# A decoder layer on one core: q and b of the input projection computed as units with the activation in the array, and the gates on the same activation

## The chip, the cores and the metric

The kernel runs on one core of one Trainium2 chip. TensorE (PE) multiplies; VectorE (DVE) and ScalarE (ACT) prepare its operands and take its results out of the accumulators; SyncE (SP) and GpSimd (POOL) issue transfers. A matmul holds a block of 128 by 128 of one operand in the array (the stationary one) and streams the other past it (the moving one). The metric is the device time of one execution in microseconds; 2173.79 us is the median of three runs of the kernel before (2173.52 to 2174.09).

## What is computed

One decoder layer on 256 tokens with 16 learned meta tokens ahead of them (272 rows of 2048 values), all in float32:

```python
s = s + 0.5 * swiglu_ffn(rms_norm(s, norm_ffn1), ffn1_w_gu, ffn1_w_down)
h = rms_norm(s, norm_mix)
q, k, v, b_gate, c_gate, u = split(h @ w_in)            # 6 x 1024 columns
y_att  = rms_norm(softmax(q1 k1) v - lam * softmax(q2 k2) v, subln)   # 8 heads, causal
y_conv = b_gate * conv3(c_gate * u)
gates  = sigmoid(h @ w_gate)                             # 2 x 2048 columns
s = s + (gates[0] * (y_att @ w_branch[0]) + gates[1] * (y_conv @ w_branch[1])) @ w_out
s = s + 0.5 * swiglu_ffn(rms_norm(s, norm_ffn2), ffn2_w_gu, ffn2_w_down)
return rms_norm(s, norm_final)[16:]
```

## The kernel before

Every float32 operand of a large product is split into a high part, which the fast float32 form of the array takes exactly, and a low remainder: ACT casts the high part (`wh` of a weight tile), DVE subtracts it (`wl`). A product is then three matmuls: high by high, high by low, low by high.

There are two forms of a linear layer. In the dense form, `linear`, a weight block of 128 by 128 is stationary and the activation streams: 272 columns in three matmuls where the meta tokens are needed (k, v and the first feed-forward part), 258 columns (c and u), or for 256 tokens one matmul of 512 columns (both parts of the activation side by side) and one of 256 (q, b and the output projection). One call covers 512 output columns: 16 chunks of 128 rows by 4 blocks, 192 or 128 matmuls. In the unit form, `linear_mix`, activation blocks of 128 tokens are stationary and 512 columns of weights stream. A unit covers 1024 output columns and goes through eight pairs of chunks. A pair of kind D takes two tiles of 12 matmuls. A pair of kind S saves an eighth: it uses sums of activation blocks (`Mixed.combine`, kept in the tiles `sp`) and of weight blocks (the tiles `t`, lines 566 to 568) and takes 21 matmuls in four tiles. The plan "DDDSDSDS" of the gates has 5 x 24 + 3 x 21 = 183 matmuls. The results of a unit have tokens on the partitions; where the next step wants channels there, 128 by 128 blocks are transposed back on TensorE (`back`).

The order of the mixer before: k, q, v for heads 0 to 3, k, q, v for heads 4 to 7 (dense calls), then c, u, b twice, then four times a unit of gates and `z`, the product with the branch weights. The gates need an activation of 256 tokens in blocks of 128. Its normed copy `hn` is made chunk by chunk during u and b of the second half (`renorm`, lines 462 to 476), with the sums of its three S pairs.

Work that is not part of a layer's own stream stands in lists. `side` holds steps that a linear pops at fixed chunks (`side_at`): the 18 attention steps, their norm, the eight output transposes, the second half of the convolution. An attention step for one head and one half of the tokens does three things (lines 816 to 866): `values` of the unit two back, `turn` (transposes on TensorE) of the unit one back, `scores` of its own, whose softmax then runs through DVE, ACT and DVE and must be done when the next step transposes it. `pending` holds the evaluation of the layer before, run at chunk 1 of the next one; `later` holds transposes back. The written order is then put through a scheduler that interleaves each engine's instructions; each engine runs its own list in order. SP loads weight tiles of 1 MB into a ring of four (`st`), and `wh` and `wl` have rings of three tiles, so ACT and DVE prepare a tile at most three ahead of TensorE. The eight PSUM banks are one pool.

SBUF: one pool of 24 buffers of 4352 bytes (tag `act`) holds the activations, the attention's tensors and held weights. The pool `sc` has two buffers of 2176 bytes, for softmax tiles, sums and single 512-column weight tiles of the S pairs. The addresses of one of its two buffers are 128 bytes away, modulo 256, from those of all other streamed weight tiles, and the first tile (`wh`) of each S pair's single product lies there.

## Time and profile before

| | |
|---|---|
| median of the runs (lowest to highest) | 2173.79 us (2173.52 to 2174.09) |
| the profiled execution, its own time | 2175.27 us |
| its span, first to last instruction | 2173.5 us |
| mean granted clock of TensorE | 0.998 |
| busy: PE, DVE, ACT, POOL | 99%, 71%, 50%, 4% |

The stages of the profiled execution, from the first matmul of each name to the first of the next:

| stage | from us | to us |
|---|---|---|
| first feed-forward part | 7.0 | 810.1 |
| k, q, v of heads 0 to 3 | 810.1 | 881.2 |
| k, q, v of heads 4 to 7 | 881.2 | 964.3 |
| c, u, b, first half | 964.3 | 1048.4 |
| c, u, b, second half | 1048.4 | 1118.7 |
| gates and z, four times | 1118.7 | 1375.2 |
| output projection | 1375.2 | 1467.7 |
| second feed-forward part and the end | 1467.7 | 2173.5 |

How to read the lines: in a view of groups, a row has the line of the kernel, the engine, the operation, the tile written and the tiles read, the shapes, the count, the total and the mean time of one, then the idle time just before and what ended it. In a timeline a row has start, length and instruction. In a table of windows it has the stretch, its length and the busy time and number of instructions of each engine; PEld is TensorE's weight load, which runs beside the matmuls. Instructions overlap a little at their ends, so what one costs in a packed row is the distance between starts, which is less than its length.

### The profile page before, as it was taken

To read this page: it belongs to the slowest core of one execution; us is meant where nothing else is said; L and a number is where in the kernel's file an instruction comes from. 1 tells how busy PE (TensorE), PEld (TensorE's weight loads), DVE (VectorE), ACT (ScalarE), POOL (GpSimd) and SP (SyncE) were. 2 spreads that over 40 slices of the span, in tenths; PEclk is the share of its full clock that TensorE was granted. 3 is DMA by queue.
4 is the path that set the end of the run, shared out by engine and by line. 5 is a ranking of instruction groups with operands and counts; after the bars stand their busy time and mean duration, and the time that the engine had idled before them with its cause. 6 is when DMAs were issued, how large, how long until landed. Compare 5 with 4: busy or idle time off the path is not lost.

```text
span 2173.5 us, 33436 instructions
## 1 busy us (share of the span) xinstructions
PE 2161.5 (99%) x13459; PEld 1961.4 (90%) x13459; DVE 1553.4 (71%) x2060; ACT 1082.9 (50%) x1366; POOL 82.5 (4%) x93
## 2 busy tenths in 40 slices
PE   9999999999999999999999999999999999999998
PEld 9999999999999999999988888888888888888886
DVE  7555554445555555567897778678998899988997
ACT  6343343333433444445555555456665566555664
POOL 0000000000000000000000000001110111002100
PEclk9999999999999999999999999999999999999999
DMA  7555555555555555544556567557886999779964
GB/s 248 181 175 175 175 178 175 175 175 175 175 175 175 175 175 175 175 137 138 182 184 202 197 200 222 197 183 232 272 253 207 275 290 281 231 222 290 285 222 155
DMA packets 209313, 440.77 MB, mean 203 GB/s; under 512 B 10557, under 2 KB 11270, under 8 KB 209158
## 3 DMA queue, kind: packets, MB, share of 16 engines
q1 hardware_dynamic: 192214, 398.13, 54.7%
q0 software_dynamic: 16480, 39.85, 8.4%
q8 instruction: 105, 1.72, 0.3%
q10 hardware_dynamic: 464, 0.66, 0.1%
q14 instruction: 50, 0.41, 0.1%
HBM read 431.26 MB, written 2.10 MB: 199 GB/s over the span
## 4 chain that ended last, share of the span: by engine, by line
PE 96%; DVE 2%; DMA 1%; issue 1%; ACT 0%; POOL 0%; SPq 0%; DVEq 0%; ACTq 0%; POOLq 0%
PE pg L528 6%; PE pg L529 6%; PE pg L530 6%; PE pu L323 4%; PE pd L321 4%; PE pd L323 4%; PE pu L321 4%; PE pg L323 4%; PE pu L322 4%; PE pd L322 4%; PE pg L321 4%; PE pg L322 4%; PE o L319 3%; PE g L528 2%; PE g L529 2%; PE g L530 2%
## 5 line engine op out<-in xcount | busy, mean ns | idle before, releaser
L310 DVE TENSOR_TENSOR wl<-st,wh 128x1024 fp32r<-128x1024 f32 (+1 forms) x393 | 479.5, 1222 | 439.4 <-ACT wh L305 438.5
L305 ACT CAST wh<-st 128x1024 fp32r<-128x1024 f32 (+1 forms) x392 | 411.1, 1049 | 603.8 <-PE pd L322 147.2
L424 DVE TENSOR_TENSOR wl<-st,wh 128x1024 fp32r<-128x1024 f32 (+1 forms) x360 | 402.3, 1124 | 59.0 <-ACT wh L423 56.9
L423 ACT CAST wh<-st 128x1024 fp32r<-128x1024 f32 (+1 forms) x360 | 341.8, 974 | 195.5 <-PE pdx L529 45.0
L423 ACT CAST wh<-t 128x1024 fp32r<-128x1024 f32 x130 | 135.8, 1052 | 182.6 <-DVE t L568 114.3
L321 PE MATMUL pg<-h,wh 128*128 128x272 f32 x704 | 203.6, 290 | 1.2 <-ACT h L193 1.2
L321 PE MATMUL pu<-h,wh 128*128 128x272 f32 x704 | 203.1, 289 | 0.0
L321 PE MATMUL pd<-m,wh 128*128 128x272 f32 x704 | 203.1, 288 | 0.0
L323 PE MATMUL pd<-m,wl 128*128 128x272 f32 x704 | 203.0, 288 | 0.0
L323 PE MATMUL pu<-h,wl 128*128 128x272 f32 x704 | 203.0, 288 | 0.0
L322 PE MATMUL pg<-h,wh 128*128 128x272 f32 x704 | 202.5, 288 | 0.1
L322 PE MATMUL pu<-h,wh 128*128 128x272 f32 x704 | 202.4, 288 | 0.0
L322 PE MATMUL pd<-m,wh 128*128 128x272 f32 x704 | 202.4, 288 | 0.0
L323 PE MATMUL pg<-h,wl 128*128 128x272 f32 x704 | 201.7, 290 | 0.2 <-DVE wl L310 0.2
L424 DVE TENSOR_TENSOR wl<-t,wh 128x1024 fp32r<-128x1024 f32 x130 | 158.1, 1223 | 48.1 <-ACT wh L423 43.2
L529 PE MATMUL pg<-wh,h 128*128 128x512 f32 x399 | 156.3, 392 | 0.0
L530 PE MATMUL pg<-wl,h 128*128 128x512 f32 x399 | 156.1, 391 | 0.0
L528 PE MATMUL pg<-wh,h 128*128 128x512 f32 x399 | 155.7, 390 | 0.0
L321 PEld LDWEIGHTS pg<-h,wh 128*128 128x128 f32 x704 | 132.7, 189 | 2.0 <-ACT h L193 1.4
L322 PEld LDWEIGHTS pg<-h,wh 128*128 128x128 f32 x704 | 133.2, 189 | 0.4 <-DVE h L194 0.4
L323 PEld LDWEIGHTS pg<-h,wl 128*128 128x128 f32 x704 | 132.1, 189 | 0.8 <-DVE wl L310 0.6
L322 PEld LDWEIGHTS pu<-h,wh 128*128 128x128 f32 x704 | 132.7, 189 | 0.0
(327 smaller groups left out, 4880.4 us busy)
## 6 DMA issues: line engine op xcount, KB each, us to landing
st<-in_ffn_w_gu_dram SPq DMA_DIRECT2D x183, 512.0 KB, 5.8
st<-in_ffn_w_down_dram SPq DMA_DIRECT2D x88, 1024.0 KB, 5.2
st<-in_ffn_w_gu_dram SPq DMA_DIRECT2D x84, 1024.0 KB, 5.1
st<-in_w_in_dram SPq DMA_DIRECT2D x48, 1024.0 KB, 5.1
st<-in_w_gate_dram SPq DMA_DIRECT2D x64, 512.0 KB, 4.6
t<-in_ffn_w_gu_dram POOLq DMA_DIRECT2D x64, 512.0 KB, 6.8
st<-in_w_branch_dram SPq DMA_DIRECT2D x32, 512.0 KB, 5.4
st<-in_w_out_dram SPq DMA_DIRECT2D x16, 1024.0 KB, 5.1
```

What stands on the lines that cost most here:

```text
L305: nc.scalar.copy(out=wh[:, :m, :], in_=sw)
L310: nc.vector.tensor_sub(wl[:, :m, :], sw, wh[:, :m, :].bitcast(F32))
L319: nc.tensor.matmul(acc[j][:, : 2 * n], wh[:, i, f], act.both(c, t0, t1), start=first, stop=False)
L321: nc.tensor.matmul(a, wh[:, i, f], act.part(c, 0, t0, t1), start=first, stop=False)
L322: nc.tensor.matmul(a, wh[:, i, f], act.part(c, 1, t0, t1), start=False, stop=False)
L323: nc.tensor.matmul(a, wl[:, i, f], act.part(c, 0, t0, t1), start=False, stop=last)
L423: part_last[:] = [nc.scalar.copy(out=wh, in_=src).ins]
L424: part_last.append(nc.vector.tensor_sub(wl, src, wh.bitcast(F32)).ins)
L528: nc.tensor.matmul(ps[k], hi, wh, start=first, stop=False)
L529: nc.tensor.matmul(ps[k], lo, wh, start=False, stop=False)
L530: nc.tensor.matmul(ps[k], hi, wl, start=False, stop=left[k] == 0)
```

## The change

Five things are changed together.

1. q and b are no longer four dense calls of 512 columns. Each is one unit of 1024 columns, run after the first k in the order q, b, with the gates' plan of pairs (`Q_B`). The unit's results have tokens on the partitions. They are transposed back in eight sets of four 128 by 128 transposes (`turned_back`): q's four during b, b's four during the v that follows. q's norm factor moves into the scores' scale (`rq`), b's into four ACT multiplications. A norm factor with tokens on the partitions is made for it (`end_tok`).
2. The gates and the two new units read `h2`, the activation that k, v, c and u stream. `renorm` and `hn` go. The sums of the three S pairs are made from `s` while the feed-forward part ends. The sigmoid gets the norm factor as its scale.
3. Addresses: each piece of `h2` has 320 columns, of which the last 272 are used, so that the token blocks start 256 bytes into a piece, at the same residue modulo 256 as the weight tiles. `sc` gets buffers of 2304 bytes and `lam` is padded to 192 bytes, so that both buffers of `sc` lie at that residue too. The 24 buffers become 16 of 4352 bytes and 8 of 5120 bytes (tag `big`).
4. The attention has fewer dense calls to stand in. Five steps each stand in the second k and the second v, three chunks apart; in c and u they are three chunks apart as before. The output transposes are done two heads at a time.
5. What b's call evaluated, the product with the convolution, follows the convolution's second half: in c of the second half, and in the first pair of the first gates.

The second half of the w_in stage is thus k, v, c, u, c, u.

In TensorE's list, where q begins. Names: `h` is the activation, `wh` and `wl` the weight parts, `q`, `qx` and `k` PSUM banks. Before:

```order
L323 MATMUL k_8521<-h_131,wl 128x272
L319 MATMUL q_8790<-h_124,wh 128x512
L323 MATMUL q_8790<-h_124,wl 128x256
L319 MATMUL q_8791<-h_124,wh 128x512
L323 MATMUL q_8791<-h_124,wl 128x256
```

In the changed kernel, at the same place:

```order
L331 MATMUL k_8544<-h_131,wl 128x272
L522 MATMUL q_8855<-wh,h_124 128x512
L523 MATMUL q_8855<-wh,h_124 128x512
L524 MATMUL q_8855<-wl,h_124 128x512
L522 MATMUL q_8859<-wh,h_124 128x512
L523 MATMUL q_8859<-wh,h_124 128x512
```

and further on in b, where the first part of q is turned back (`qb_ps` is its bank):

```order
L523 MATMUL bx<-wh,h_125 128x512
L524 MATMUL bx<-wl,h_125 128x512
L780 MATMUL qb_ps<-ident,cgate 128x128 x4
L522 MATMUL b_9183<-wh,h_125 128x512
L523 MATMUL b_9183<-wh,h_125 128x512
```

Where a matmul of 512 and one of 256 columns stood for each weight block, three of 512 stand for each pair of an activation block and 512 weight columns, and sets of four transposes stand between them.

In DVE's list, a wide attention unit (272 columns of scores) in the second dense call after the first v (before, q of heads 4 to 7), the softmax between `sc_ps` and `rs`:

```order
L826 SCALAR_TENSOR_TENSOR sc<-sc_ps,mask 128x272 x2
L830 TENSOR_REDUCE mx<-sc 128x2
L837 RECIPROCAL rs<-sm 128x2
L838 TENSOR_TENSOR rs<-rs,lam 128x1
L839 TENSOR_SCALAR sc<-sc,rs 128x272
L840 SCALAR_TENSOR_TENSOR sc<-sc,rs 128x272
L310 TENSOR_TENSOR wl<-st,wh 128x1024
```

and the first wide unit of the changed kernel, in the second k:

```order
L846 SCALAR_TENSOR_TENSOR sc<-sc_ps,rq,mask 128x272 x2
L850 TENSOR_REDUCE mx<-sc 128x2
L318 TENSOR_TENSOR wl<-st,wh 128x1024
L857 RECIPROCAL rs<-sm 128x2
L858 TENSOR_TENSOR rs<-rs,lam 128x1
L859 TENSOR_SCALAR sc<-sc,rs 128x272
L860 SCALAR_TENSOR_TENSOR sc<-sc,rs 128x272
```

A weight tile's subtraction has moved into the middle of the softmax.

In DVE's list at the head of the first gates (`yv` and `cg` belong to the convolution, `yc` is the split result, `t` the weight sums of the first S pair). Before:

```order
L950 TENSOR_TENSOR yv_11087<-half,yv_11087 128x256 x2
L187 TENSOR_TENSOR yc_10131<-yv_11087,yc_10131 128x2x256
L424 TENSOR_TENSOR wl<-st,wh 128x1024
L187 TENSOR_TENSOR yc_10132<-yv_11087,yc_10132 128x2x256
L424 TENSOR_TENSOR wl<-st,wh 128x1024
L566 TENSOR_TENSOR t_12023<-st 128x1024
```

In the changed kernel:

```order
L963 SCALAR_TENSOR_TENSOR yv_11253<-cg,vec,yv_11253 128x256
L970 TENSOR_TENSOR yv_11253<-yv_11253,bT_9556 128x1024
L432 TENSOR_TENSOR wl<-st,wh 128x1024
L195 TENSOR_TENSOR yc_10535<-yv_11253,yc_10535 128x2x256
L195 TENSOR_TENSOR yc_10536<-yv_11253,yc_10536 128x2x256
L560 TENSOR_TENSOR t_11935<-st 128x1024
```

b's evaluation has gone from this place; the whole convolution of the second half (taps of four channel groups, L959 to L963) and its product with `bT` stand there now, ahead of the same weight sums.

The diff, cut to its core:

```diff
-N_ACT = 24
+N_ACT = 16
+N_BIG = 8
+PIECE = 320
...
-GATES = ("DDDSDSDS", 2, {(2, 1): 3, (4, 1): 5, (6, 1): 7}, ())
-FFN2_FIRST = ("DDDDSSDS", 1, {(3, 0): 4, (3, 1): 5, (6, 0): 7}, (4, 5))
-FFN2 = ("DDSDSSDS", 1, {(1, 1): 2, (3, 0): 4, (3, 1): 5, (6, 0): 7}, (2, 4, 5))
-DOWN_FIRST = ("DDDDDDSD", 1, {(5, 1): 6}, ())
-DOWN = ("DDSDSDSD", None, {(1, 1): 2, (3, 1): 4, (5, 1): 6}, ())
-DOWN_LAST = ("DDDSDS", 1, {(2, 1): 3, (4, 1): 5}, ())
+GATES = ("DDDSDSDS", (2,), {(2, 1): 3, (4, 1): 5, (6, 1): 7}, ())
+Q_B = ("DDDSDSDS", (1, 2), {(2, 1): 3, (4, 1): 5, (6, 1): 7}, ())
...
-    lam = const.tile([P, 1], F32, name="lam")
+    lam = const.tile([P, 48], F32, name="lam")[:, 0:1]
...
     class Act:
-        def __init__(self, name, chunks, width):
-            self.width = width
-            self.tiles = [
-                apool.tile([P, 2, 2, width], F32R, tag="act", name=f"{name}{g}") for g in range(chunks // 2)
-            ]
+        def __init__(self, name, chunks, width, wide_slots=(), piece=None):
+            self.width, self.lead = width, 0 if piece is None else piece - width
+            self.tiles = []
+            for g in range(chunks // 2):
+                if g in wide_slots:
+                    w = piece or width
+                    raw = apool.tile([P, 4 * PIECE], F32R, tag="big", bufs=N_BIG, name=f"{name}{g}")
+                    self.tiles.append(raw[:, : 4 * w].rearrange("p (c l w) -> p c l w", c=2, l=2))
+                else:
+                    self.tiles.append(apool.tile([P, 2, 2, width], F32R, tag="act", name=f"{name}{g}"))
         def both(self, c, t0, t1):
-            return self.tiles[c // 2][:, c % 2, :, t0:t1]
+            return self.tiles[c // 2][:, c % 2, :, self.lead + t0 : self.lead + t1]
         def part(self, c, lo, t0, t1):
-            return self.tiles[c // 2][:, c % 2, lo, t0:t1]
+            return self.tiles[c // 2][:, c % 2, lo, self.lead + t0 : self.lead + t1]
...
-    def total(ps, n):
-        if 2 * n > 512:
-            return ps[:, :n]
-        b = tmp.tile([P, SEQ], F32, tag="half", name="half")
-        nc.scalar.copy(out=b[:, :n], in_=ps[:, n : 2 * n])
-        nc.vector.tensor_add(b[:, :n], ps[:, :n], b[:, :n])
-        return b[:, :n]
...
-        def renorm(self, p, norm, kind):
-            f = tmp.tile([P, 2, SEQ], F32, tag="sc", name="hnf")
-            for k in range(2):
-                c = 2 * p + k
-                nc.vector.scalar_tensor_tensor(
-                    out=f[:, k, :], in0=s(c, NMETA), scalar=col(self.g0 + c), in1=norm.rstd[:, NMETA:],
-                    op0=ALU.mult, op1=ALU.mult,
-                )
-            tl = apool.tile([P, 2, 2, SEQ], F32R, tag="act", name=f"hn{p}")
-            self.act.tiles.append(tl)
-            nc.scalar.copy(out=tl[:, :, 0, :], in_=f)
-            nc.vector.tensor_sub(tl[:, :, 1, :], f, tl[:, :, 0, :].bitcast(F32))
-            if kind == "S":
-                self.combine(p, f)
+            self.t0 = act.width - SEQ
...
-            return [self.act.part(c, lo, i * P, (i + 1) * P) for lo in range(2)]
+            t0 = self.t0 + i * P
+            return [self.act.part(c, lo, t0, t0 + P) for lo in range(2)]
...
-            if p == turn_at and later:
+            if p in turn_at and later:
...
-    h1 = Act("h1", DC, T)
+    h1 = Act("h1", DC, T, range(NH))
...
-    h2 = Act("h2", DC, T)
+    h2 = Act("h2", DC, T, range(NH), PIECE)
     norm2 = Norm(0, "2")
+    hm = Mixed(h2, G_MIX, True)
...
-            side.append(norm2.end)
+            side.extend((norm2.end, norm2.end_tok))
+        if c % 2 and GATES[0][c // 2] == "S":
+            side.append(lambda p=c // 2: hm.sum(p))
...
-    def qk_evict(dst, g, n0, nm):
+    def k_evict(g):
         def f(ps):
-            tl = apool.tile([P, GC, T - n0], F32, tag="act", name=f"{nm}T{g}")
+            kT[g] = apool.tile([P, GC, T], F32, tag="act", name=f"kT{g}")
             for j in range(GC):
-                nc.vector.tensor_mul(tl[:, j, :], total(ps[j], T - n0), norm2.rstd[:, n0:])
-            dst[g] = tl
+                nc.vector.tensor_mul(kT[g][:, j, :], ps[j][:, :T], norm2.rstd)
         return f
+    def turned_back(dst, v, k):
+        pt = bank("qb_ps")
+        for c in range(2):
+            for i in range(2):
+                nc.tensor.transpose(
+                    pt[:, (2 * c + i) * P : (2 * c + i + 1) * P], v[:, i, (2 * k + c) * P : (2 * k + c + 1) * P], ident
+                )
+        nc.scalar.copy(out=dst[:, 2 * k : 2 * k + 2, :].rearrange("p c t -> p (c t)"), in_=pt)
+    def q_end(*halves_):
+        nc.vector.tensor_scalar_mul(rq, norm2.rtok, HD**-0.5)
+        for g, v in enumerate(halves_):
+            qT[g] = apool.tile([P, GC, SEQ], F32, tag="act", name=f"qT{g}")
+            later.extend(lambda g=g, v=v, k=k: turned_back(qT[g], v, k) for k in range(2))
+    def b_end(*halves_):
+        for g, v in enumerate(halves_):
+            for i in range(2):
+                nc.scalar.mul(v[:, i, :], v[:, i, :], norm2.rtok[:, i : i + 1])
+            bT[g] = apool.tile([P, GC, SEQ], F32, tag="act", name=f"bT{g}")
+            later.extend(lambda g=g, v=v, k=k: turned_back(bT[g], v, k) for k in range(2))
...
-            sc = tmp.tile([P, 2, T], F32, tag="sc", name="sc")
+            sc = tmp.tile([P, 2, T + NMETA], F32, tag="sc", name="sc")
...
-                    out=sc[:, c, :nk], in0=ps[:, :nk], scalar=HD**-0.5, in1=mask[:, T - nk :], op0=ALU.mult, op1=ALU.add
+                    out=sc[:, c, :nk], in0=ps[:, :nk], scalar=rq[:, qt : qt + 1], in1=mask[:, T - nk :], op0=ALU.mult, op1=ALU.add
...
-    def att_out(h):
+    def att_out(h0):
         def f():
-            g, j = h // GC, h % GC
-            if j == 0:
+            g, j0 = h0 // GC, h0 % GC
+            if j0 == 0:
                 yf[g] = wide([P, GC, SEQ], "yf")
             pt = bank("yt")
-            for qt in range(2):
-                o = oN[g][:, qt, j, :]
-                nc.vector.tensor_scalar_mul(o, o, ors[:, qt * NH + h : qt * NH + h + 1])
-                nc.tensor.transpose(pt[:, qt * P : (qt + 1) * P], o, ident)
-            nc.vector.tensor_scalar_mul(yf[g][:, j, :], pt[:, :SEQ], subg)
-            if j == GC - 1:
+            for k in range(2):
+                for qt in range(2):
+                    o = oN[g][:, qt, j0 + k, :]
+                    nc.vector.tensor_scalar_mul(o, o, ors[:, qt * NH + h0 + k : qt * NH + h0 + k + 1])
+                    nc.tensor.transpose(pt[:, (2 * k + qt) * P : (2 * k + qt + 1) * P], o, ident)
+            nc.vector.tensor_scalar_mul(yf[g][:, j0 : j0 + 2, :].rearrange("p c t -> p (c t)"), pt, subg)
+            if j0 + 2 == GC:
...
-        linear(h2, allk, w_in, 0, W2 + g * GW, 0, T, "k", qk_evict(kT, g, 0, "k"))
-        linear(h2, allk, w_in, 0, g * GW, NMETA, T, "q", qk_evict(qT, g, NMETA, "q"))
-        linear(h2, allk, w_in, 0, 2 * W2 + g * GW, 0, T, "v", v_evict(g))
+        dense = dict(side_at=(2, 5, 8, 11, 14)) if g else {}
+        linear(h2, allk, w_in, 0, W2 + g * GW, 0, T, "k", k_evict(g), **dense)
+        if g == 0:
+            mixed(Q_B, hm, w_in, (0, GW), "q", q_end)
+            mixed(Q_B, hm, w_in, (3 * W2, 3 * W2 + GW), "b", b_end)
+            dense = dict(later_at=(3, 5, 7, 9))
+        linear(h2, allk, w_in, 0, 2 * W2 + g * GW, 0, T, "v", v_evict(g), **dense)
...
-            side.extend(att_out(h) for h in range(NH))
+            side.extend(att_out(h) for h in range(0, NH, 2))
...
+            def product():
+                taps(2)
+                nc.vector.tensor_mul(yv, yv, bT[g])
+                split(yc, g, yv)
...
-            side.insert(0, lambda: taps(2))
-        def b_evict(ps, yv=yv, g=g):
-            for j in range(GC):
-                nc.vector.tensor_mul(yv[:, j, :], yv[:, j, :], norm2.rstd[:, NMETA:])
-                nc.vector.tensor_mul(yv[:, j, :], total(ps[j], SEQ), yv[:, j, :])
-            split(yc, g, yv)
...
+            side.insert(0, product)
         kw = dict(side_at=(3, 6, 9, 12))
         linear(h2, allk, w_in, 0, 4 * W2 + g * GW, n0, T, "c", c_evict, **kw)
-        for i, (m0, t0, nm, evict) in enumerate(((5 * W2, n0, "u", u_evict), (3 * W2, NMETA, "b", b_evict))):
-            if g == 1:
-                def after(k, i=i):
-                    if k in (4, 7, 10, 13):
-                        p = 4 * i + k // 3 - 1
-                        hg.renorm(p, norm2, GATES[0][p])
-                kw["after"] = after
-            linear(h2, allk, w_in, 0, m0 + g * GW, t0, T, nm, evict, **kw)
-    while side:
-        side.pop(0)()
-    mg = Act("mg", DC, SEQ)
+        linear(h2, allk, w_in, 0, 5 * W2 + g * GW, n0, T, "u", u_evict, **kw)
+    mg = Act("mg", DC, SEQ, range(4, NH))
...
-                nc.scalar.activation(v, v, AF.Sigmoid)
+                for i in range(2):
+                    nc.scalar.activation(v[:, i, :], v[:, i, :], AF.Sigmoid, scale=norm2.rtok[:, i : i + 1])
...
-        mixed(GATES, hg, w_gate, [br * D + d * GW for br in range(2)], "g", g_end)
+        mixed(GATES, hm, w_gate, [br * D + d * GW for br in range(2)], "g", g_end)
+        while side:
+            side.pop(0)()
```

32 lines of the change are left out of this document (22 added, 10 removed).

## The prediction

> **What bounds the kernel now.** I read the page's busy time first, then TensorE's waits, then a table of windows over the stages that the change touches, last the timelines of the places it loads. The first two views are these (in the second, total, times and longest wait in us):
>
> ```profile
> PE 2161.5 (99%) x13459; PEld 1961.4 (90%) x13459; DVE 1553.4 (71%) x2060; ACT 1082.9 (50%) x1366; POOL 82.5 (4%) x93
> ...
> engine line waited for: us in total, times, longest us
> PE pg L321 <- ACT h L193: 1.2, 1, 1.2
> PE warm L79 <- DVE ones L73: 1.1, 1, 1.1
> PE pd L363 <- DVE wl L424: 0.5, 1, 0.5
> PE pd L361 <- ACT wh L423: 0.3, 1, 0.3
> PE pg L323 <- DVE wl L310: 0.2, 1, 0.2
> ```
>
> TensorE is busy for 99% of the span, and its waits come to 3.3 us, of which 2.5 stand in the prologue. No wait lies between 834 and 1375 us, where this change works. So the time is the number of matmuls by the distance between their starts, plus whatever new wait the change makes. The windows give both (length, busy time and count of PE, PEld, DVE, ACT, POOL, granted clock, DMA share, GB/s):
>
> ```profile
> 834.60:857.10 22.50, 22.50 (x131) 19.63 (x130) 11.06 (x13) 9.11 (x10) 0.00 (x0) 1.00 0.57 188
> 857.10:881.20 24.10, 24.10 (x195) 24.10 (x194) 12.77 (x18) 8.95 (x10) 0.00 (x0) 1.00 0.53 175
> 935.30:964.30 29.00, 29.00 (x230) 27.58 (x229) 20.41 (x42) 14.21 (x36) 0.00 (x0) 1.00 0.46 151
> 1096.00:1118.70 22.70, 22.70 (x133) 19.84 (x132) 22.53 (x44) 13.40 (x18) 0.00 (x0) 1.00 0.54 174
> 1118.70:1160.20 41.50, 41.50 (x185) 34.30 (x184) 35.83 (x46) 23.62 (x28) 0.00 (x0) 1.00 0.64 209
> 1182.10:1224.60 42.50, 42.50 (x192) 35.12 (x191) 34.78 (x37) 22.88 (x27) 0.00 (x0) 1.00 0.60 198
> ```
>
> In this order they are the first dense q, the first v, the second v with its attention steps, the last dense b, the first unit of gates, and the second one, in which two sets of four transposes stand. PE fills each of them at full clock.
>
> **The units.** A dense call of q costs 22.5 us, and b 22.7 with the few side matmuls that stand in it. A unit does the work of two such calls in 41.5. Four dense calls go: 4 x 22.5 = 90.0. Two units come: 2 x 41.5 = 83.0. That is -7.0. I set the windows' edges to the nearest tenth or half, and an edge off by 0.05 counts four times in the first product and twice in the second. I take -6.8, with -6.4 and -7.2 as ends. The units' other engines are not late: in the gates' window DVE is busy for 35.8 and ACT for 23.6 of 41.5 us, and no attention step stands in q or b. Their 1024 columns of weights come through SP's queue in the order of use, as the gates' do, with a DMA share of 0.64, and the gates never waited for a load. Of the other transfers only the last norm's few move ahead in POOL's queue, and POOL is busy for 4%. So I cost these at nothing; if the ring ran dry, a tile would be late by up to its landing time, 5.1 us or 4.6:
>
> ```profile
> st<-in_w_in_dram SPq DMA_DIRECT2D x48, 1024.0 KB, 5.1
> st<-in_w_gate_dram SPq DMA_DIRECT2D x64, 512.0 KB, 4.6
> ```
>
> **The transposes.** What dense calls did for nothing, the units need: eight sets of four transposes, q's in b and b's in the first v. One set in the second gates, and the matmul after it:
>
> ```profile
> 1195.71 0.60 PE L665 MATMUL mt_ps<-ident,cgate 128*128 128x128 f32 x4
> 1196.06 0.48 PE L528 MATMUL g<-wh,hn 128*128 128x512 f32 x1
> ```
>
> From start to start a set takes 0.35 us, and the matmul behind it is longer than its like. The windows say the rest: 42.5 against 41.5 us is 0.50 for each set. The low end is 8 x 0.35 = 2.8, the high end 8 x 0.50 = 4.0; I take 0.475, near the windows, because they hold the after-effect: +3.8. The ACT copies that empty the banks stand on an engine that is half idle (22.9 of 42.5 us).
>
> The same transposes as a group, and the group that the small matmuls below rest on:
>
> ```profile
> L665 PE MATMUL mt_ps<-ident,cup 128*128 128x128 f32 x88 | 14.9, 272 | 0.0
> L230 PE MATMUL ssq_ps<-ones,ssq 128*128 128x1 f32 x4 | 0.5, 229 | 0.0
> ```
>
> The first of these rows has 272 ns from start to end of one transpose. Four of them one after another would take 1.09 us, but the timeline has four started and ended within 0.60. The Trainium skill, "TensorE: Matmul & The Clock Gate", Part 4 (PE-mode transpose), gives about 275 ns for a transpose as one kernel saw it; charged singly, the eight sets would by that page cost an estimated 8.8 us instead of 3.8. The duration agrees with the row above, the single charging does not agree with the timeline.
>
> **Small matmuls.** `end_tok` makes the norm factor with tokens on the partitions. Before, it runs once, for the second feed-forward part, and has the one-column products of the row of L230, 0.5 us together. One more call is worth 0.5 if nothing overlaps and nothing if all does: +0.3. The scale `rq` is one small DVE instruction.
>
> **The addresses of `sc`.** The first S pair of gates has a single tile out of the odd buffer. Its neighbours in the timeline:
>
> ```profile
> 1135.02 0.40 PE L528 MATMUL g<-wh,sp 128*128 128x512 f32 x1
> ...
> 1135.94 0.39 PE L529 MATMUL g<-wh,hn 128*128 128x512 f32 x1
> ...
> 1137.08 0.39 PE L528 MATMUL g<-wh,sp 128*128 128x512 f32 x1
> 1137.53 0.39 PE L530 MATMUL g<-wl,sp 128*128 128x512 f32 x1
> 1137.98 0.39 PE L529 MATMUL g<-wh,hn 128*128 128x512 f32 x1
> ```
>
> The first two rows are four matmuls apart: 0.92 us. The last three are also four apart from first to last: 0.90. So the tile from the odd buffer costs some 0.02 us more (0.00 to 0.04 with the rounding). The plans have 65 S pairs outside q and b (12 in the gates, 43 and 10 in the second feed-forward part): 65 x 0.02 = 1.3. That the address is the cause isn't shown, only that these are the tiles. I take -0.9, with -1.3 and 0 as ends.
>
> **Moved work on DVE.** At the head of the first gates stood b's evaluation; now the second half's last convolution taps and the product stand there. Before:
>
> ```profile
> 1095.49 0.75 DVE L935 TENSOR_TENSOR cg<-u,cg 128x258 f32<-128x258 f32 x2
> ...
> 1098.26 0.76 DVE L935 TENSOR_TENSOR cg<-u,cg 128x258 f32<-128x258 f32 x2
> ...
> 1101.04 1.23 DVE L310 TENSOR_TENSOR wl<-st,wh 128x1024 fp32r<-128x1024 f32 x1
> ...
> 1118.82 0.42 DVE L949 TENSOR_TENSOR yv<-yv,rstd 128x256 f32<-128x256 f32 x1
> ...
> 1126.89 0.69 DVE L187 TENSOR_TENSOR yc<-yv,yc 128x512 fp32r<-128x512 f32 x1
> ...
> 1127.97 1.23 DVE L424 TENSOR_TENSOR wl<-st,wh 128x1024 fp32r<-128x1024 f32 x1 [0.39 <-ACT wh L423]
> ...
> 1134.47 1.22 DVE L424 TENSOR_TENSOR wl<-t,wh 128x1024 fp32r<-128x1024 f32 x1 [1.20 <-ACT wh L423]
> ```
>
> Half a set of taps takes 2.77 us (1095.49 to 1098.26, and again to 1101.04). The head now holds two halves (5.5), a product over 1024 columns (about 1.2, as `wl`) and two splits (1.2): 7.9. Before it held the stretch 1118.82 to 1127.58, less three `wl` in it (3.4): 5.3. So DVE is 2.6 us later at the S pair, less its idle 0.39. The weight remainder made at 1134.47 is done at 1135.69 and first read at 1137.53 (row above): 1.84 us of room. Then 2.6 - 0.39 - 1.84 = 0.4 us of wait, once. The ends are 0 and 1.0 (DVE idles 1.20 us before that tile too, for ACT, which is late next if DVE is). I take +0.4. Behind this tile all further `wl` queue, but a 41.5 us unit has 5.7 us of idle DVE to recover in.
>
> **At nothing.** `renorm`, its splits and its sums leave the second half of u and b; they lay under PE, so no time comes back. The new sums at the end of the first feed-forward part have the slack of DVE there, which in the neighbouring v is 11.3 of 24.1 us. The sigmoid's scale adds one ACT instruction for each tile on an engine half idle. Output transposes two heads at a time are the same 16, in four sets of four instead of eight of two: -0.2 to 0. The prologue's reordering stands beside waits of 2.5 us in all; I put it at 0, with -1.2 (the whole wait on `h`) and +1.2 (one more like it).
>
> **Sum.** -6.8 + 3.8 + 0.3 - 0.9 + 0.4 = -3.2. No row prices the banks of PSUM that the eight sets take; I leave 0.2 for them: -3.0. Against the profiled execution's own 2175.27 that gives 2172.3, with a span of 2170.5 instead of 2173.5. The median of the runs is 1.5 below the profiled execution, so the forecast is 2173.8 - 3.0 = 2170.8. That is -0.14%. About 0.2% (4.35 us) is what a measurement of this kernel can tell from no change: 2169.4 to 2178.1.
>
> **Rivals.** *The softmax becomes late* (the slower side). An attention step has three chunks of a dense call for its softmax. In the second u of before, its end is tight:
>
> ```profile
> 1001.24 0.78 DVE L826 SCALAR_TENSOR_TENSOR sc<-sc_ps,mask 128x272 f32<-128x272 f32 x2
> ...
> 1003.97 0.17 DVE L837 RECIPROCAL rs<-sm 128x2 f32<-128x2 f32 x1 [1.19 <-ACT sc L833]
> ...
> 1004.76 0.50 DVE L840 SCALAR_TENSOR_TENSOR sc<-sc,rs 128x272 f32<-128x272 f32 x1
> ...
> 1005.45 0.27 PE L848 MATMUL aT<-ident,sc 128*16 128x128 f32 x1
> ```
>
> The softmax starts on DVE at 1001.24; its result stands at 1005.26 (1004.76 + 0.50) and TensorE takes it at 1005.45: 0.19 us of room. A matmul of the first v takes 24.1 / 192 = 0.1255 us; with 258 columns instead of 272 it is an estimated 0.120 in u. The 36 matmuls of a step then give k and v 0.2 us more room, about 0.38. The changed order puts one `wl` (1.14 to 1.23 us) into this chain. If all of it came on top, 8 wide steps would lose 4 x (1.14 - 0.38) + 4 x (1.14 - 0.19) = 6.8 us: 2177.6. Against it: DVE idles 1.19 us at exactly that place, waiting for ACT's exponential, and that would hide the tile. It decides from a growth of about 0.66 us a step on (8 x 0.66 less 2.3 of room is 3.0). I give it 0.14.
>
> *The one address helps the dense calls too.* All 32 blocks of `h2` now start at the weights' residue. Before, the blocks' own means differ:
>
> ```profile
> L322 PE MATMUL k<-h,wh x128: 282/288/291, 810.2 to 908.0; 128*128 128x272 f32 x128
> L322 PE MATMUL u<-h,wh x128: 278/283/292, 993.3 to 1095.8; 128*128 128x258 f32 x128
> ```
>
> If all took the low end, half of 768 matmuls of k and v would win 6 ns and half of 768 of c and u 5 ns: 4.2 us, so 2166.6. Against it: the first v's 192 matmuls fill 24.1 us, 125.5 ns each, whatever the block. I give it 0.14.
>
> *Transposes cost their own 272 ns.* 32 x 0.272 = 8.7 instead of 3.8 is +4.9, so 2175.7. The distance of 0.35 us and the windows speak against it. 0.04. *The rest* (a new wait in the prologue or elsewhere that I don't see): 0.06, half of it above 2178.1.
>
> **Numbers.** The forecast's own case holds 0.62, with 2168.5 to 2172.5 as its own range and a fifth of it below 2169.4. Faster by over 0.2%: 0.14 from the second rival and 0.12 from the tail, 0.26. Slower by over 0.2%: half of the first rival (a second `wl` in the chain) and 0.03 of the rest, 0.10. Within: 0.64. The range 2166.6 to 2177.0 leaves out some 0.07 above and 0.08 below.
>
> **What would show it.** Two windows of 41.5 us where q and b are, the second with 2 us more for its transposes. S pairs whose first tile has starts 0.90 us apart. No wait of TensorE on `sc` between 900 and 1070 us; one under 1 us on `wl` or `wh` in the first gates. If waits on `aT` or `sc` come eight times, the first rival holds. I am wrong if a unit in w_in takes over 42.5 us apart from its transposes, or if TensorE waits for `wl` throughout the attention stretch, where DVE had 20.4 of 29.0 us to do.

## The result and the profile after the change

The changed kernel takes 2171.02 us (median of 20 runs, 2170.36 to 2173.38). The kernel before, measured beside it, takes 2173.99 (20 runs, 2173.07 to 2175.47). The ratio is 0.9986, with a 95% interval of 0.998 to 0.9993: 3.0 us faster, as forecast to 0.2 us. That is inside the 0.2% that the prediction counted as no change, though the interval leaves out 1.

The page's busy time, and the view of TensorE's waits, of the changed kernel:

```profile
PE 2156.0 (99%) x13349; PEld 1952.7 (90%) x13349; DVE 1567.5 (72%) x2054; ACT 1092.1 (50%) x1379; POOL 82.9 (4%) x93
```

```profile
engine line waited for: us in total, times, longest us
PE pd L362 <- DVE wl L432: 1.7, 2, 1.2
PE warm L82 <- DVE ones L76: 1.1, 1, 1.1
PE pg L329 <- ACT h L201: 0.7, 1, 0.7
PE pd L360 <- ACT wh L431: 0.3, 1, 0.3
PE pg L329 <- ACT wh L313: 0.3, 1, 0.3
PE c L331 <- DVE wl L318: 0.2, 1, 0.2
```

In this view TensorE still never waits in the middle of the layer, apart from 0.2 us in c. It is a view of the matmuls: a wait that stops only the weight load ahead of a matmul is not in it, and one such wait, on a softmax, turns up further down. The first row is new: before, the waits on a remainder (`wl`) in the last product `pd` came to 0.5 us once, now to 1.7 in two. A table of windows over the stages that the change touches, in the columns of the prediction's table:

```profile
833.06:874.54 41.48, 41.48 (x186) 34.35 (x184) 31.53 (x34) 21.96 (x25) 0.00 (x0) 1.00 0.62 203
874.54:918.08 43.54, 43.54 (x201) 35.84 (x199) 36.10 (x40) 24.04 (x29) 0.00 (x0) 1.00 0.59 193
918.08:943.86 25.78, 25.75 (x209) 25.53 (x208) 15.82 (x19) 12.46 (x16) 0.00 (x0) 1.00 0.50 164
974.07:1005.50 31.43, 31.43 (x252) 29.36 (x250) 23.93 (x54) 17.06 (x49) 0.00 (x0) 1.00 0.40 130
1113.73:1155.44 41.71, 41.71 (x185) 34.28 (x184) 37.79 (x50) 22.93 (x27) 0.00 (x0) 1.00 0.60 202
1177.33:1219.78 42.45, 42.45 (x193) 35.13 (x191) 34.77 (x37) 23.08 (x27) 0.00 (x0) 1.00 0.60 198
```

They are the units of q and b, the first v, the second v, and the first two units of gates. q takes 41.48 us, b 2.06 more for its four sets of transposes. The second gates take 42.45 where they took 42.51.

The distances between the first matmuls of the stages, in us, of two executions of each kernel (the second ones belong to the first two experiments below):

| stage | before | again | changed | again |
|---|---|---|---|---|
| first feed-forward part | 803.05 | 802.15 | 801.50 | 801.50 |
| k, q, v, c, u, b | 308.60 | 308.58 | 305.28 | 305.29 |
| gates and z | 256.54 | 256.54 | 256.61 | 256.64 |
| output projection | 92.49 | 92.49 | 92.48 | 92.49 |
| second feed-forward part, to its last product | 630.63 | 630.66 | 629.98 | 629.98 |
| the last product (`pd`), to the start of its last matmul | 66.33 | 66.84 | 67.59 | 68.53 |

The stages in the middle repeat to 0.03 us. The first and the last row vary by up to 1 us between executions; this is why the two profiles first compared differ by 4.3 us in span (2173.5 and 2169.2) where the medians differ by 3.0.

### The profile page after: what moved, and what is told of

Same layout as the page of the kernel before. It is cut to its first block, busy times and chain, and to the rows that moved or that the text cites. A ratio compares the mean times of both kernels' runs of the same rounds, so it can differ in the third digit from the quotient of the medians.

```text
span 2169.2 us, 33235 instructions
## 1 busy us (share of the span) xinstructions
PE 2156.0 (99%) x13349; PEld 1952.7 (90%) x13349; DVE 1567.5 (72%) x2054; ACT 1092.1 (50%) x1379; POOL 82.9 (4%) x93
## 4 chain that ended last, share of the span: by engine, by line
PE 96%; DVE 2%; DMA 1%; ACT 1%; issue 0%; POOL 0%; SPq 0%; DVEq 0%; ACTq 0%
PE pg L524 6%; PE pg L522 6%; PE pg L523 6%; PE pu L331 4%; PE pd L331 4%; PE pd L329 4%; PE pu L329 4%; PE pu L330 4%; PE pd L330 4%; PE pg L331 4%; PE pg L329 4%; PE pg L330 4%; PE o L327 3%; PE pd L522 2%; PE pd L523 2%; PE pd L524 2%
## 5 line engine op out<-in xcount | busy, mean ns | idle before, releaser
L431 ACT CAST wh<-t 128x1024 fp32r<-128x1024 f32 x142 | 148.3, 1053 | 206.2 <-DVE t L562 135.4
L432 DVE TENSOR_TENSOR wl<-t,wh 128x1024 fp32r<-128x1024 f32 x142 | 172.7, 1224 | 57.8 <-ACT wh L431 52.8
L330 PEld LDWEIGHTS pd<-m,wh 128*128 128x128 f32 x704 | 132.7, 189 | 0.0
```

Source lines behind the costliest of these rows:

```text
L330: nc.tensor.matmul(a, wh[:, i, f], act.part(c, 1, t0, t1), start=False, stop=False)
L431: part_last[:] = [nc.scalar.copy(out=wh, in_=src).ins]
L432: part_last.append(nc.vector.tensor_sub(wl, src, wh.bitcast(F32)).ins)
```

## The experiments

All of them ran beside the kernel before, whose medians in the four comparisons were 2174.15, 2174.18, 2174.06 and 2174.06. Times are set against these, or against the 2171.45 us of the changed kernel's own repeat.

### Both kernels again

No edit.

> The kernel before, once more, for a second profile of it. In the two profiles compared so far the first stage (the first gate product of the first feed-forward part) takes 31.05 us before and 29.50 after, and the span differs by 4.3 us where the medians differ by 3.0. Theory 1: the 1.5 us of the first stage are chance of that one execution. Then this profile shows 29.5 to 30.2 us there, and a span of about 2172.2. Theory 2: the changed order of the prologue is worth it. Then this profile shows 31.0 again.

> The changed kernel, once more, as the partner of the others on this chip: 3.0 us faster than before (-2.5 to -3.4). Its profile should again show units of q and b of 41.5 and 43.5 us, a first stage of 29.5, and one wait of 1.2 us on a weight remainder near the end, which the profile of before did not have. If that wait is chance it is gone here.

The kernel before gave 2174.24 us (ratio 1.0, 0.9991 to 1.0009), the changed one 2171.45 (0.9988, 0.9979 to 0.9996). The first stage of the kernel before took 30.14 us this time, that of the changed one 29.49 as before. So 0.9 of the 1.55 us were chance, and about 0.65 seem not to be: the four profiles of kernels with the old layout of pools have 30.1 to 31.1 there, and all those with the new one 29.5 to 29.9. Why is left open; no run took the order of the prologue alone. The wait near the end came again, 1.2 us on the same remainder.

### The addresses of sc

The kernel before with two edits:

```diff
-            sc = tmp.tile([P, 2, T], F32, tag="sc", name="sc")
+            sc = tmp.tile([P, 2, T + NMETA], F32, tag="sc", name="sc")
-    lam = const.tile([P, 1], F32, name="lam")
+    lam = const.tile([P, 48], F32, name="lam")[:, 0:1]
```

> The kernel before with the addresses of sc alone changed (buffers of 2304 bytes, lam padded), so that both buffers stand at the weights' residue modulo 256. Theory 1 (130 matmuls whose two operands had different residues cost some 7 ns each): gates units with transposes take 42.45 instead of 42.51, the second feed-forward part 0.65 us less, together -0.9 us. Rival (the address has no part in it): the windows are unchanged and the time is the same within 0.3.

2174.12 us (0.9999, 0.999 to 1.0008): no gain. But the S pairs did gain (42.45 us for a unit of gates), and it was given back. The windows of the output projection, before and here:

```profile
1375.19:1467.68 92.49, 92.49 (x541) 81.11 (x540) 65.83 (x109) 47.55 (x66) 0.00 (x0) 1.00 0.54 182
```

```profile
1373.41:1466.87 93.46, 93.46 (x541) 81.50 (x540) 66.01 (x109) 47.52 (x66) 0.00 (x0) 1.00 0.53 180
```

TensorE is busy in the whole of both, so its matmuls themselves were slower. By the addresses of the built kernels, the padding of `lam` had here moved every large tile behind it from residue 224 modulo 256 to 128. In the changed kernel, with its other new small tiles beside the same padding, they are at 224 as before. (The traces hold no addresses: every residue given here is that of the built program.) So the next run left `lam` alone:

```diff
-            sc = tmp.tile([P, 2, T], F32, tag="sc", name="sc")
+            sc = tmp.tile([P, 2, T + NMETA], F32, tag="sc", name="sc")
```

> The kernel before with the buffers of sc at 2304 bytes and nothing else, so that both of them, and every weight tile, stand at residue 224 modulo 256. (The run before this one, with lam padded too, moved every tile to residue 128: the S pairs won 0.9 us, but the output projection took 93.46 us instead of 92.49.) Theory 1: the gates' units again take 42.45 instead of 42.51, the second feed-forward part 0.8 us less, the output projection stays at 92.49, and the time falls by 0.9 to 1.0. Rival: the output projection lost its time to the alignment of sc itself; then it takes 93.46 here too and the time stays.

2173.35 us against 2174.18 (0.9996, 0.9988 to 1.0005), 0.8 less, and in the trace:

```profile
1181.03:1223.48 42.45, 42.45 (x192) 35.14 (x191) 34.76 (x37) 22.88 (x27) 0.00 (x0) 1.00 0.61 198
1373.94:1466.42 92.48, 92.48 (x542) 81.14 (x541) 65.82 (x110) 47.56 (x66) 0.00 (x0) 1.00 0.54 182
```

The gates' units take 0.06 us less each (0.24 together), the second feed-forward part up to its last product 629.99 instead of 630.63 and 630.66: some -0.65. The sum, -0.9, is the term of the prediction. The four products `z` between the gates take 0.15 us more together, so the stages as a whole gain about 0.7. By its interval the time alone would not show it; the windows, which repeat to 0.03 us, do.

### The addresses of h2

The lists of all engines stay the same; only the place of the 272 columns within a piece of 320 moves:

```diff
-            self.width, self.lead = width, 0 if piece is None else piece - width
+            self.width, self.lead = width, 0 if piece is None else 16
```

> The changed kernel with h2's token blocks 128 bytes further, at residue 96 where the weight tiles have 224. Nothing else moves, and the lists of all engines are the same. Theory 1 (a matmul whose two operands differ in residue costs 7 to 10 ns more): 882 matmuls of q, b and the gates are now such, so +6 to +9 us against the changed kernel, units of 42.5 us or more instead of 41.5. Rival A (only a change of residue from one matmul to the next costs): a few pairs, +0.5. Rival B (of the prediction: the one address helps the dense calls of k, v, c and u): these become slower by up to 4 us; by theory 1 they stay at 24.6, 25.8, 30.2 and so on, because their moving operand always stood at another residue.

2177.87 us (1.0018, 1.0009 to 1.0027): 6.4 more than the changed kernel, and 3.7 more than the kernel before. Windows of q and of the first and second k, then of the first k in the changed kernel, then the group of q's matmuls, here and in the changed kernel:

```profile
833.59:876.08 42.49, 42.49 (x185) 34.48 (x184) 31.71 (x34) 22.01 (x25) 0.00 (x0) 1.00 0.61 198
808.38:833.59 25.21, 25.21 (x201) 25.13 (x199) 20.67 (x42) 13.52 (x20) 0.00 (x0) 1.00 0.50 167
946.39:977.09 30.70, 30.65 (x239) 28.66 (x238) 19.78 (x39) 15.51 (x33) 0.00 (x0) 1.00 0.45 145
```

```profile
808.45:833.06 24.61, 24.61 (x201) 24.53 (x199) 20.55 (x42) 13.53 (x20) 0.00 (x0) 1.00 0.53 171
```

```profile
L522 PE MATMUL q<-wh,h x39: 390/393/405, 833.6 to 874.0; 128*128 128x512 f32 x39
L522 PE MATMUL q<-wh,sp x12: 389/389/396, 850.3 to 875.4; 128*128 128x512 f32 x12
```

```profile
L522 PE MATMUL q<-wh,h x39: 389/389/389, 833.1 to 872.5; 128*128 128x512 f32 x39
L522 PE MATMUL q<-wh,sp x12: 389/389/389, 849.4 to 873.9; 128*128 128x512 f32 x12
```

q takes 1.01 us more, b 0.70, the four gates 0.77 to 0.92 each. The matmuls that read h2 are longer by 4 ns in the median, those of the sums `sp` (which did not move) hardly. From start to start the medians are 232 against 227 ns, and the mean distance of those in q that read h2 grows by 6. So the first theory holds for the units, with 5 to 6 ns a matmul instead of 7 to 10, and rival A falls. But the dense calls changed too, which this theory had excluded: the first k takes 25.21 us instead of 24.61, the second 30.70 instead of 30.20, while c and u stay within 0.05. So the residue matters to dense calls of 272 columns as well, and here it was the wrong one (32 instead of 160). Of the longer time, the units have some 5.2 us and the four calls of k and v 2.0.

### q and b dense again

```diff
-            mixed(Q_B, hm, w_in, (0, GW), "q", q_end)
-            mixed(Q_B, hm, w_in, (3 * W2, 3 * W2 + GW), "b", b_end)
-            dense = dict(later_at=(3, 5, 7, 9))
+            for dst, c0, nm in ((qT, 0, "q"), (bT, 3 * W2, "b")):
+                for j in range(2):
+                    linear(h2, allk, w_in, 0, c0 + j * GW, NMETA, T, nm, dense_evict(dst, j, nm))
```

> The changed kernel with q and b as four dense calls again (in the order q, q, b, b, after the first k), each with its evaluation as before and without the eight sets of transposes; the rest stays. By the prediction's terms: 4 x 22.45 - 2 x 41.5 = +6.8, less 3.8 for the transposes, so +3.0 against the changed kernel, about the time of before. Rival: the gain came from elsewhere (the steps of the attention, which lie in fewer calls); then the time stays within 1 us of the changed kernel.

2174.23 us (1.0001, 0.9992 to 1.001): 2.8 more than the changed kernel, near the 3.0 of the terms. The windows of q (both calls) and of the first v, which here has no transposes:

```profile
833.23:878.44 45.21, 45.21 (x259) 39.27 (x257) 23.67 (x29) 18.79 (x22) 0.00 (x0) 1.00 0.57 186
923.67:947.35 23.68, 23.68 (x194) 23.68 (x193) 12.70 (x17) 8.94 (x10) 0.00 (x0) 1.00 0.55 178
```

Two things differ from the prediction's rows. A dense call of q now takes 22.6 us instead of 22.44, so that against these calls the two units gain 7.5 and not 6.8. And the v takes 23.68 instead of the 24.11 of the kernel before, with the same 192 matmuls: 123.3 instead of 125.6 ns each. In the changed kernel the median distance of starts has fallen likewise in all four calls of k and v, from 125 or 126 to 124 ns. That is a gain of 0.43 us in each, hidden in its first v by the transposes.

### The transposes twice

The eight sets of four are each done a second time, at places of their own (q's additional ones in b's fourth pair):

```diff
-            later.extend(lambda g=g, v=v, k=k: turned_back(qT[g], v, k) for k in range(2))
+            later.extend(lambda g=g, v=v, k=k: turned_back(qT[g], v, k) for k in (0, 0, 1, 1))
...
-            dense = dict(later_at=(3, 5, 7, 9))
+            dense = dict(later_at=(3, 4, 5, 6, 7, 8, 9, 10))
```

> The changed kernel with each of the eight sets of four transposes done twice, at places of its own. By the prediction's price of 0.475 for a set: +3.8 us against the changed kernel. If a transpose costs its own 272 ns: 32 x 0.272 = +8.7. If the sets were hidden under something: 0.

2174.90 us (1.0006, 0.9997 to 1.0015): 3.45 more than the changed kernel. Windows of b and the first v:

```profile
874.34:920.03 45.69, 45.69 (x217) 37.27 (x216) 36.76 (x41) 26.36 (x33) 0.00 (x0) 1.00 0.55 184
920.02:947.30 27.28, 27.28 (x225) 27.27 (x224) 15.19 (x18) 14.91 (x20) 0.00 (x0) 1.00 0.47 155
```

They have 2.15 and 1.50 us more, 3.65 together, 0.46 for a set. A charge of 272 ns for each transpose (8.7 us) is excluded. In the Trainium skill, "TensorE: Matmul & The Clock Gate", Part 4 (PE-mode transpose), the 275 ns are the length of one transpose in one kernel. The trace agrees with that length (272 ns) and shows besides that the next one starts long before it ends: four start and end within 0.60 us.

### The order of the end

The new wait stands here in TensorE's timeline of the changed kernel (start, length, instruction, wait and what ended it):

```profile
2144.44 0.50 PE L362 MATMUL pd<-wl,m 128*128 128x512 f32 x1 [0.53 <-DVE wl L432]
...
2147.32 0.50 PE L362 MATMUL pd<-wl,m 128*128 128x512 f32 x1 [1.21 <-DVE wl L432]
```

and DVE's timeline has four remainders in a row behind one piece of the final norm:

```profile
2143.16 1.23 DVE L432 TENSOR_TENSOR wl<-st,wh 128x1024 fp32r<-128x1024 f32 x1 [4.01 <-ACT wh L431]
2144.31 0.68 DVE L1128 TENSOR_TENSOR sT<-sT,gfin 128x512 f32<-128x512 f32 x1
2144.91 4.62 DVE L432 TENSOR_TENSOR wl<-st,wh 128x1024 fp32r<-128x1024 f32 x4
```

By the order of the built program, the first of these four belongs to a tile that TensorE uses last but one, and the second is the one it waits for. The kernel before has the same instructions in the order of use:

```profile
2148.79 2.36 DVE L424 TENSOR_TENSOR wl<-st,wh 128x1024 fp32r<-128x1024 f32 x2 [3.91 <-ACT wh L423]
2151.07 0.69 DVE L1114 TENSOR_TENSOR sT<-sT,gfin 128x512 f32<-128x512 f32 x1
2151.67 3.49 DVE L424 TENSOR_TENSOR wl<-st,wh 128x1024 fp32r<-128x1024 f32 x3
```

The written program is the same there; what changed is the pool that each held tile comes from (`held_tile`), and with it the order that the scheduler made. The edit only exchanges which four of the twelve held tiles use the new pool:

```diff
-        if len(held_tiles) <= 8:
+        if len(held_tiles) > 4:
```

> The changed kernel, with one change: of the twelve weight tiles held for the very last product, the first four instead of the last four lie in the new pool of 5120 byte buffers. That changes no work, but the order in which the last casts and remainders stand in the lists of ACT and DVE, which is then the order of their use. Theory 1 (the new wait of 1.2 us near the end comes of a remainder that stands behind a later one): -1.2 to -2.0 us against the changed kernel, 4.2 to 5.0 below before. Rival (DVE is late there by as much in any order): the wait moves to another tile and the time stays.

2168.98 us (0.9975, 0.9965 to 0.9985): 2.5 less than the changed kernel, more than the theory's 1.2 to 2.0. TensorE's waits are then:

```profile
PE warm L82 <- DVE ones L76: 1.1, 1, 1.1
PE pg L329 <- ACT h L201: 0.8, 1, 0.8
PE pt L686 <- DMA xin<-in_x_dram: 0.3, 1, 0.3
PE c L331 <- DVE wl L318: 0.2, 1, 0.2
```

The view has no wait in the last product any more, also not the older one on ACT's cast. A likely reason for the latter is that ACT's order changed too: two of the last five casts now stand ahead of its table load (2138.69 and 2141.10, the load at 2142.15), where all five stood behind it (the load at 2140.69, the casts from 2142.10). The last product takes 65.89 us instead of 67.59 and 68.53.

### The softmax nearer to its limit

```diff
-        dense = dict(side_at=(2, 5, 8, 11, 14)) if g else {}
+        dense = dict(side_at=(2, 4, 6, 8, 10)) if g else {}
```

> The changed kernel with the five attention steps in the second k and the second v two chunks apart instead of three. This puts the rival of the late softmax to the point where it should decide: a step then has 24 x 0.124 = 3.0 us of matmuls and 1.3 of its own for a softmax that takes about 4.0 on DVE and ACT, plus a weight remainder or two of 1.1 to 1.2. Theory 1 (three chunks are enough because the remainder falls into DVE's idle time, two are not): waits of TensorE on the softmax of 0.3 to 1.5 us at about half of the ten steps, +2 to +6 us. Rival (the softmax has far more room than its shortest margin showed): no waits, the same time within 0.5.

2172.66 us (0.9995, 0.9985 to 1.0004): 1.2 more than the changed kernel, less than expected. TensorE waits for the softmax now, but little. The transposes of a step hold `sc` in the array, so a late softmax can stop the weight load alone, and the view of the weight loads has to be read too:

```profile
PE aT L868 <- DVE sc L860: 0.4, 2, 0.3
```

```profile
PEld aT L868 <- DVE sc L860: 1.2, 3, 0.5
```

These are five waits in ten steps, as many as theory 1 expected, but of 0.1 to 0.5 us instead of 0.3 to 1.5. In TensorE's list the steps do not stand where they were written, 24 dense matmuls apart: the first transposes have 36, 24 and 70 between them, and in the changed kernel, where 36 were written, 28, 36 and 48. Where the scheduler sets a step further back, its softmax gets more time; that this is why the waits stayed small is not shown. So there is a limit near two chunks, and its price was put too high. In the changed kernel itself, the first wide unit's softmax looks like this on DVE, and TensorE's use of it:

```profile
962.92 1.22 DVE L318 TENSOR_TENSOR wl<-st,wh 128x1024 fp32r<-128x1024 f32 x1
964.07 0.17 DVE L857 RECIPROCAL rs<-sm 128x2 f32<-128x2 f32 x1
...
964.86 0.50 DVE L860 SCALAR_TENSOR_TENSOR sc<-sc,rs 128x272 f32<-128x272 f32 x1
```

```profile
965.42 0.28 PE L868 MATMUL aT<-ident,sc 128*16 128x128 f32 x1
```

```profile
965.42 0.09 PEld L868 LDWEIGHTS aT<-ident,sc 128*16 128x16 f32 x1 [0.33 <-DVE sc L860]
```

The remainder that moved into the chain has taken the place of the idle 1.19 us ahead of the reciprocal. The result stands at 965.36, and the weight load that starts at 965.42 has waited 0.33 us for it, so this softmax was late by about 0.3 us. It is the only one of the 16 in the changed kernel. The kernel before has one too, in its first b:

```profile
1039.23 0.09 PEld L848 LDWEIGHTS aT<-ident,sc 128*16 128x16 f32 x1 [0.36 <-DVE sc L840]
```

So the late softmax costs the change nothing on balance.

### The first feed-forward part at the better address

The two runs on h2 and on dense q and b had shown dense calls of 272 columns at 23.68 us, 24.11 or more, by the address alone. The first feed-forward part consists of such calls, over blocks whose residues run through 32, 96, 160 and 224. Its input can have h2's layout in the space that it already holds:

```diff
-    h1 = Act("h1", DC, T, range(NH))
+    h1 = Act("h1", DC, T, range(NH), PIECE)
```

> The changed kernel with h1, the activation of the first feed-forward part, laid out as h2 is (pieces of 320 columns, the last 272 used), so that every block that the first feed-forward part's gate and up products stream starts at residue 160 modulo 256, 64 below the weights' 224; so far its blocks start at 32, 96, 160 and 224 in turn. Nothing else moves, the lists of all engines are the same. Theory 1 (the runs so far: a call of 192 matmuls over h2 at residue 160 takes 23.68 us, over blocks of mixed residues 24.11, at residue 32 24.3 or more): 22 such calls gain 0.43 us each, -9.5 us against the changed kernel. Rival (the shorter v in the run with dense q and b came of something else at that place): the calls stay at 24.11 and the time too.

2162.66 us (0.9947, 0.9934 to 0.9959): 8.8 less than the changed kernel. The third call of the first feed-forward part, in the changed kernel and here:

```profile
60.75:84.86 24.11, 24.11 (x195) 24.11 (x193) 12.53 (x15) 9.75 (x11) 0.00 (x0) 1.00 0.52 175
```

```profile
60.12:83.80 23.68, 23.68 (x195) 23.68 (x193) 12.52 (x15) 9.67 (x11) 0.00 (x0) 1.00 0.55 179
```

Twenty-one of the 22 calls lose 0.41 to 0.43 us (the first, in the prologue, loses 0.03); the part takes 792.52 us instead of 801.50. The eleven calls of its down product read `m`, whose blocks keep the four residues, and take 265.6 us as before. By the same 0.43 us a call they would gain an estimated 4.7 us; no run tried it.

Then a version with three layouts changed, that of h1, that of the end, and mg, the activation of the output projection, 192 bytes further:

```diff
-    mg = Act("mg", DC, SEQ, range(4, NH))
+    mg = Act("mg", DC, SEQ, range(4, NH), shift=48)
```

> The changed kernel with three layouts changed: h1 as in the run before this one, the held weight tiles as in the run on the order of the end, and mg (moving operand of the output projection, 512 columns) 192 bytes further, at residue 160 instead of 224. Expected: -9.5 for h1, -2.4 for the end, and for mg 256 matmuls of 229 instead of 232 ns, -0.8: about 2158.5 us, 0.7% under before. Rival for mg (the row of 229 in the dense q of before belongs to the other residue in turn): the output projection stays at 92.48 us.

2160.84 us (0.994, 0.9927 to 0.9952). h1 and the end came as expected, but the output projection took 93.51 us instead of 92.48: the guess from the dense q was wrong. Without the edit of mg:

> The changed kernel with h1 at residue 160 and the held tiles' other pools, and mg left as it was (the run before moved mg, and its output projection took 93.51 us instead of 92.48). Theory (the terms add up): -9.0 for h1, -2.4 for the end, so 1.0 under the run before: about 2159.7 us, 0.66% under before. Rival (the run before was slower than its terms for another cause, for its stages sum to 10.4 us less than the changed kernel's and not 11.3): the time stays at 2160.8.

2159.70 us (0.9933, 0.992 to 0.9947): 14.4 us less than the kernel before and 11.8 less than the changed one. That it is to the tenth what the terms gave is chance, since the changed kernel's own two medians differ by 0.4.

## Why the prediction was right, and where it was not

**The units.** q takes 41.48 us and b 41.48 without its transposes, against 4 x 22.44: -6.80, the term as put. It had a premise that the prediction did not name: the rows of 41.5 were of gates on `hn`, at the weights' residue, and the units now read h2. With h2 128 bytes off, the change would have lost 3.7 us instead of gaining 3.0; most of that difference lies in the units.

**The transposes.** +3.8 was forecast. b has 2.06 for its sets, and v 25.78 against 23.68, so 2.10: together +4.16; done a second time they cost +3.65. Against the old v (24.11) the second half would have looked like 1.67.

**The dense calls.** This is the step that failed: "the first v's 192 matmuls fill 24.1 us, 125.5 ns each, whatever the block". That mean was taken over a mix of four residues and could not tell what one of them costs. In the trace of before, the medians by place in the piece and matmul are 124 to 127 ns; with all blocks at 160 the mean is 123.3. The second rival had this half right: k and v gained 0.43 us in each of four calls, -1.7, where it had put -2.3 for them; c and u, whose time hardly changed with h2's residue, gained little (median distances of 120 ns before, 119 to 120 after). But the residue that helps is not the weights': the 272 columns start at 160, 64 below the weights' 224, and only their last 256 begin at 224.

**sc.** -0.9 forecast, -0.9 in the windows of the S pairs' stages, of which the products z give 0.15 back. In the first gates the starts that were to show it are 0.90 us apart (1130.09 to 1130.99). The cause, which the prediction left open, is the address.

**The head of the first gates.** +0.4 forecast; 41.71 against the 41.52 that the aligned `sc` alone gives is +0.19. The chain waited as described. DVE idled 1.20 us for the cast ahead of the same remainder, and the matmul that reads it came late:

```profile
1131.36 2.36 DVE L432 TENSOR_TENSOR wl<-t,wh 128x1024 fp32r<-128x1024 f32 x2 [1.20 <-ACT wh L431]
```

```profile
1132.35 0.39 PE L523 MATMUL g<-wh,sp 128*128 128x512 f32 x1
1132.64 0.50 PE L524 MATMUL g<-wl,sp 128*128 128x512 f32 x1
1132.98 0.39 PE L522 MATMUL g<-wh,h 128*128 128x512 f32 x1
```

Its start and the next are 0.29 and 0.34 us after the one ahead, where 0.23 is usual: 0.17 late in all.

**Small matmuls and side steps.** The first k, whose call itself gained 0.43, takes 24.61 after 24.56, so `end_tok` is about +0.5, the upper end. What is left of the stage is +0.56 (-6.80 + 4.16 - 1.72 + 0.48 + 0.56 = -3.32): the attention steps and output transposes, which I had at nothing, with the 0.2 of wait in c, less what c and u gained. The 0.2 that I left for the PSUM banks would be in there too; no run shows it by itself.

**Where a cost was put at nothing.** The last product was not in the prediction at all, since no line of its program changed. It lost 1.2 us to a new wait. With the older one on ACT's cast, which varies, the four profiles of the table are 0.8 to 2.2 us apart; all profiles with the old order have 66.3 to 66.8 us there, those with the new one 67.6 to 68.7. The prologue, put at 0 with 1.2 on both sides, gained about 0.65.

So the sum came out by two errors of opposite sign: about -2.4 that were not counted (dense calls, prologue) against +0.8 to +2.2 at the end, 0.4 more for the transposes and 0.7 for the small steps. The range covers this; the closeness to 0.2 us is luck.

**The rivals.** The late softmax did not come eight times, for the reason given against it: the remainder fell into the idle time. It came once, by 0.3 us, so the sign "no wait of TensorE on `sc`" was missed by one. The kernel before had one as well, at 1039 us: the reading that no wait lies between 834 and 1375 us was made from the matmuls alone and left out the weight loads. Transposes at 272 ns each are excluded by two runs.

## What to carry to other kernels

When a kernel is bound by one engine's instructions, ask for the distance between their starts by operand address, not for one mean: 2 ns on each of 4000 matmuls was worth more than the whole change. When pools are re-cut, compare the order of all engines to the very end, also where no line was edited. And a pad that repairs one alignment moves everything behind it, so its price is to be looked for in the other stages.

## What the runs showed of the hardware that I had not expected

- Dense matmuls of 272 columns, all blocks of the moving operand at one residue modulo 256, weights at 224: 23.68 us for 192 with residue 160 (123.3 ns each), 24.11 with the four residues in turn (125.6), and with residue 32 the first k is 0.60 us longer than with 160 (126.4 by that).
- Matmuls with 512 streamed weight columns start 227 ns apart where both operands lie at residue 224, or both at 128, and 232 where the stationary block lies at 96.
- For 512 streamed activation columns (two parts of 256) I found no rule. The output projection takes 92.49 us with both operands at 224, 93.46 with both at 128, and 93.51 with the activation at 160 and the weights at 224. Dense q, all at 224, takes 22.6 us a call, and 22.44 over blocks at 32 and 160 in turn. The two parts of the streamed activation lie 1024 bytes apart in the output projection, 1088 in q of the kernel before and 1280 in the dense q of the changed one, so the residue was not the only difference there. What in the memory or the array causes all this stays open: only the addresses were varied.
